# A longer ring of score tiles, one staging place less, and loads of single tiles, in an argmax, gather and scatter kernel

The kernel runs on **one core of one Trainium2 chip**. The metric is the device time of one execution in microseconds (us); lower is better.

## The reference

```python
B, S, H = (8, 2048, 2560)          # fp32; scores (B,S,S), values (B,S,H)
best_j = np.argmax(scores, axis=2)
gathered = values[b_idx, best_j, :].copy()
out = np.zeros_like(values)
np.add.at(out, (b_idx, best_j, slice(None)), gathered)
```

So every output row is its own row of `values`, times the number of score rows whose argmax hit it. Rows hit once are copied, rows never hit are zeroed, rows hit twice or more are gathered, scaled and scattered. No value crosses to another row.

## The kernel before

VectorE finds the argmax of each score row tile (128 rows of 2048), 16 tiles in a batch, 8 batches. TensorE counts the hits. From the counts come lists of rows, and GpSimd issues indirect DMAs from these lists: **copies** from DRAM to DRAM (16 in a batch, of some 47 real rows each), **zeros** from a row of zeros in SBUF (7 in a batch, 12 in the last), and five **gathers** into staging places, five ScalarE scalings and five **scatters**. Loads of scores go through the hardware queue (q1), all the indirect transfers through GpSimd's software queue (q0).

Score tiles go through a ring: a fixed row of places that the loads fill in turn, each as soon as VectorE has scanned the tile that lay there. Score tiles and staging places share one SBUF region, `room`. At the start the first two turns of the score ring also use most of the staging area.

```python
    R = 4; NV = 6; NX = NV * H // S; NB = 14       # NX = 7
    ZCAP, MCAP = 7, 5
    ...
    room = ctx.enter_context(nc.sbuf_tensor([P, NV * H + NB * S], FP32))
    turn = NX + NB                                 # 21 tiles
    def place(x):
        return NV * H + (x % turn - NX if x < 2 * turn else (x - 2 * turn) % NB) * S

    loads, x = {}, 0
    while x < B * NT:
        n = 1
        most_n = 1 if x < 2 or 2 * turn - 6 <= x < 2 * turn else 2 if x < 4 or 2 * turn <= x < 4 * NT else R
        while n < most_n and (x + n) % NT and place(x + n) == place(x) + n * S:
            n += 1
        loads[x] = n                               # n tiles in one DMA
        x += n
    ...
        # per batch, as soon as the counts are there:
        first = (NT, 6, 4)[min(b, 2)]              # copies that need only the counts
        for t in range(first):
            copy_once(t)
        ...                                        # the lists are made
        rest = list(range(first, NT))
        def gathers():
            for k in range(MCAP):
                v = stage()                        # next of NV staging places
                gather(v, mi[:, k:k + 1])
                nc.scalar.activation(out=v, in_=v, ..., scale=mc[:, k:k + 1])
                staged.append(v)
                if rest:
                    copy_once(rest.pop(0))
        def zeros(columns):
            for k in columns:
                scatter(zrow[:], zi[:, k:k + 1], free_running)
                if rest:
                    copy_once(rest.pop(0))
        nz = ZLAST if b == B - 1 else ZCAP
        if b == 0:
            zeros(range(nz))
            while tiles[0] < turn + NX:
                yield
            gathers()
        else:
            gathers()
            zeros(range(ZHEAD))
        for k in range(MCAP):
            scatter(staged[k], mi[:, k:k + 1], ...)
        if b > 0:
            zeros(range(ZHEAD, nz))
```

Of the kernel before, what the change touches and what calls it, by code (L numbers as in the profile page):

```python
# [10 lines left out]
FP16 = mybir.dt.float16  # L11
# [3 lines left out]
P = 128  # L15
# [21 lines left out]
def kernel(  # L37
# [7 lines left out]
    B, S, S2 = scores.shape  # L45
    _, _, H = values.shape
    assert S == S2
    NT = S // P
    BIG = float(1 << 24)
    R = 4  # L50
    G = 4
    NV = 6
    NX = NV * H // S
    NB = 14
    NM = NT // 2
    NE = 16
    LE = P // NE
# [11 lines left out]
    fin = ctx.enter_context(tc.tile_pool(name="fin", bufs=2))  # L69
    ohp = ctx.enter_context(tc.tile_pool(name="ohp", bufs=1))  # L70
# [47 lines left out]
    zrow = ctx.enter_context(nc.sbuf_tensor([P, H], FP32))  # L118
    nc.scalar.copy(zrow[:], zero1[:].to_broadcast([P, H]))


    room = ctx.enter_context(nc.sbuf_tensor([P, NV * H + NB * S], FP32))
    nc.scalar.copy(room[:, 0:NV * H - NX * S], zero1[:].to_broadcast([P, NV * H - NX * S]))
    turn = NX + NB

    def place(x):

        return NV * H + (x % turn - NX if x < 2 * turn else (x - 2 * turn) % NB) * S


    loads, x = {}, 0
    while x < B * NT:
        n = 1
        most_n = 1 if x < 2 or 2 * turn - 6 <= x < 2 * turn else 2 if x < 4 or 2 * turn <= x < 4 * NT else R
        while n < most_n and (x + n) % NT and place(x + n) == place(x) + n * S:
            n += 1
        loads[x] = n
        x += n
# [30 lines left out]
    def scatter(v, idx, note=writes_out):  # L169
        note(nc.gpsimd.indirect_dma_start(  # L170
            out=out_flat[:, :], out_offset=bass.IndirectOffsetOnAxis(ap=idx, axis=0),
            in_=v, in_offset=None, bounds_check=B * S - 1, oob_is_err=False))

    vslot = [0]
    tiles = [0]

    def stage():
        v = room[:, vslot[0] * H:(vslot[0] + 1) * H]
        vslot[0] = (vslot[0] + 1) % NV
        return v  # L180

    def count_steps(b, cnt_ps):

        am = None
        for t in range(NT):
            x = b * NT + t
            if x in loads:
                n = loads[x]
                nc.sync.dma_start(out=room[:, place(x):place(x) + n * S],
                                  in_=scores[b, t * P:(t + n) * P, :].rearrange("(p r) s -> p (r s)", r=n))  # L190
            g = t % G
            if g == 0:
                am = small.tile([P, G, 8], U32, name="am")
            rows = room[:, place(x):place(x) + S]
            mx = small.tile([P, 8], FP32)
            nc.vector.max(out=mx[:], in_=rows)  # L196
# [81 lines left out]
    def value_steps(b, cnt_ps):  # L278
# [12 lines left out]
        def copy_once(t):  # L291
            free_running(scatter_rows_in_dram(
                nc, out_flat[:, :], values[b, t * P:(t + 1) * P, :], one_i[:, t:t + 1], last_row))
# [28 lines left out]
        if b == B - 1:  # L322
# [9 lines left out]
            out=oh[:], in0=lo[:].unsqueeze(2).to_broadcast([P, NT, P]),  # L332
            in1=fill_f[:].unsqueeze(1).to_broadcast([P, NT, P]), op=ALU.is_equal)

        ez = fin.tile([P, NT, NT], FP16)
        nc.vector.tensor_tensor(  # L336
            out=ez[:], in0=hi[:, 0, :].unsqueeze(2).to_broadcast([P, NT, NT]),
            in1=lane_f[:, 0:NT].unsqueeze(1).to_broadcast([P, NT, NT]), op=ALU.is_equal)
        em = fin.tile([P, NT, NM], FP16)
        nc.vector.tensor_tensor(  # L340
            out=em[:], in0=hi[:, 1, :].unsqueeze(2).to_broadcast([P, NT, NM]),
            in1=lane_f[:, 0:NM].unsqueeze(1).to_broadcast([P, NT, NM]), op=ALU.is_equal)
        put = fin.tile([P, NT, 2 * NM + NT], FP16)
        nc.vector.tensor_tensor(out=put[:, :, 0:NM], in0=em[:], in1=row1_f[:].unsqueeze(2).to_broadcast([P, NT, NM]), op=ALU.mult)  # L344
        nc.vector.tensor_tensor(out=put[:, :, NM:2 * NM], in0=em[:], in1=cnt[:].unsqueeze(2).to_broadcast([P, NT, NM]), op=ALU.mult)
        nc.vector.tensor_tensor(out=put[:, :, 2 * NM:], in0=ez[:], in1=row1_f[:].unsqueeze(2).to_broadcast([P, NT, NT]), op=ALU.mult)  # L346
# [19 lines left out]
        def gathers():  # L366
            for k in range(MCAP):
                v = stage()
                gather(v, mi[:, k:k + 1])
                nc.scalar.activation(out=v, in_=v, func=mybir.ActivationFunctionType.Copy, bias=0.0,  # L370
                                     scale=mc[:, k:k + 1])
# [10 lines that stand above are left out]

        nz = ZLAST if b == B - 1 else ZCAP
        if b == 0:
            zeros(range(nz))

            while tiles[0] < turn + NX:
                yield
            gathers()
        else:  # L390
            gathers()
            zeros(range(ZHEAD))
        for k in range(MCAP):

            scatter(staged[k], mi[:, k:k + 1], writes_out if b * MCAP + k < B * MCAP - NV else free_running)
        if b > 0:
            zeros(range(ZHEAD, nz))
        assert not rest
# [3 lines left out]
    with tc.manual_schedule(engines={ET.PE, ET.DVE, ET.Activation, ET.SP}):  # L402
        pending = iter(())
        for b in range(B):
            cnt_ps = psum_c.tile([P, NT], FP32)
            for _ in count_steps(b, cnt_ps):
                next(pending, None)
            for _ in pending:
                pass
            pending = value_steps(b, cnt_ps)  # L410
            for _ in range((1, 4, 0)[min(b, 2)]):
                next(pending)
        for _ in pending:
            pass
        full = fin.tile([1, 2], FP32)
        nc.vector.tensor_reduce(out=full[:, 0:1], in_=tots[0:1, 0, 0:B - 1], op=ALU.max, axis=mybir.AxisListType.X)
        nc.vector.tensor_reduce(out=full[:, 1:2], in_=tots[0:1, 1, :], op=ALU.max, axis=mybir.AxisListType.X)
        over = fin.tile([1, 3], FP32)
        nc.vector.tensor_single_scalar(out=over[:, 0:1], in_=full[:, 0:1], scalar=float(ZCAP * P), op=ALU.is_gt)
        nc.vector.tensor_single_scalar(out=over[:, 1:2], in_=full[:, 1:2], scalar=float(MCAP * P), op=ALU.is_gt)  # L420
        nc.vector.tensor_single_scalar(out=over[:, 2:3], in_=most[0:1, :], scalar=float(ZLAST * LE), op=ALU.is_gt)
        over_i = fin.tile([1, 1], INT32)
        nc.vector.tensor_reduce(out=over_i[:], in_=over[:], op=ALU.max, axis=mybir.AxisListType.X)
# [69 lines left out]
```

## Time and profile before

| | before |
|---|---|
| median of three runs | 828.0 us (827.82 to 829.2) |
| profiled run | 827.44 us, span 825.6 us |
| bytes moved | 347.04 MB, 420 GB/s over the span |
| VectorE | 679.0 us busy, idle after some 697 us |

### The profile page before, as it was taken

The page shows a single profiled execution, that of the slowest core. Times are in us where ns is not written, and L with a number is a line of the kernel's source. Part 1 is how long each engine was busy: PE and PEld are TensorE (multiplying, and loading weights), DVE is VectorE, ACT ScalarE, POOL GpSimd, SP SyncE. Part 2 cuts the span into 40 slices and gives each one's busy share as a digit, 9 for nine tenths or more (in the row PEclk, how much of TensorE's full clock was granted, in tenths as well). Part 3 has the DMA queues.
Part 4 walks back from the last instruction along what each step waited for, and adds up shares of the span by engine and source line. Part 5 has one row for each costly group of instructions (what it writes and reads, how often), then busy time and mean ns, then how long its engine had stood idle before and what let it go on. Part 6 is the DMA issues. An engine that isn't in the chain of part 4 may idle for free.

```text
span 825.6 us, 2045 instructions
## 1 busy us (share of the span) xinstructions
PE 14.7 (2%) x273; PEld 14.1 (2%) x273; DVE 679.0 (82%) x794; ACT 101.2 (12%) x43; POOL 274.7 (33%) x277
## 2 busy tenths in 40 slices
PE   0000000000000000000000000000000000000000
PEld 0000000000000000000000000000000000000000
DVE  7999999999999999999999999999999996000000
ACT  2000000500220002210002300013100320230230
POOL 0000651266121260152501343501505266346351
DMA  9999999999999999999999999999999999999997
GB/s 384 432 431 429 413 409 423 392 410 413 426 429 427 423 431 431 427 424 432 420 428 429 439 419 431 419 436 430 430 415 421 425 426 423 425 427 422 424 426 313
DMA packets 45664, 347.04 MB, mean 420 GB/s; under 512 B 18742, under 2 KB 18742, under 8 KB 18742
## 3 DMA queue, kind: packets, MB, share of 16 engines
q0 software_dynamic: 38736, 212.67, 62.1%
q1 hardware_dynamic: 6912, 134.22, 38.1%
q14 instruction: 14, 0.11, 0.0%
q8 instruction: 2, 0.03, 0.0%
HBM read 354.42 MB, written 300.15 MB: 793 GB/s over the span
## 4 chain that ended last, share of the span: by engine, by line
DVE 71%; DMA 13%; issue 8%; POOL 5%; another core or an unknown queue 1%; POOLq 0%; PE 0%; DVEq 0%
DVE am L197 32%; DVE mx L196 30%; DMA room<-in_values_dram,many_i 8%; DMA out_dram<-room,many_i 4%; POOL out_dram L33 2%; DVE oh_lo L204 2%; POOL out_dram L170 2%; DVE oh L331 2%; POOL room L165 1%; DMA room<-in_scores_dram 1%; DVE lo L200 1%; DVE oh_hi L208 0%; DVE hi L202 0%; DVE put L346 0%
## 5 line engine op out<-in xcount | busy, mean ns | idle before, releaser
L196 DVE MAX8 mx<-room 128x8 f32<-128x2048 f32 x128 | 291.7, 2279 | 4.6 <-DMA room<-in_scores_dram 4.6
L197 DVE FIND_INDEX8 am<-mx,room 128x8 uint32<-128x2048 f32 x128 | 292.4, 2285 | 0.0
L370 ACT ACTIVATE room<-room,many_c 128x2560 f32<-128x2560 f32 x40 | 96.7, 2426 | 693.0 <-DMA room<-in_values_dram,many_i 693.0
L33 POOL DMA_INDIRECT out_dram<-in_values_dram,ones_i x128 | 131.2, 1025 | 145.7 <-DVE m L302 107.7
L170 POOL DMA_INDIRECT out_dram<-room,many_i x40 | 39.7, 994 | 248.2 <-ACT room L370 248.2
L165 POOL DMA_INDIRECT room<-in_values_dram,many_i x40 | 41.8, 1046 | 122.2 <-DMA out_dram<-room,many_i 73.9
L170 POOL DMA_INDIRECT out_dram<-zrow,zero_i x61 | 60.8, 996 | 18.8 <-issue 18.8
L204 DVE TENSOR_TENSOR oh_lo<-lo,lane_f 128x512 bf16<-128x512 uint32 x32 | 22.1, 692 | 0.3
L331 DVE TENSOR_TENSOR oh<-lo,fill_f 128x2048 f16<-128x2048 uint32 x8 | 18.3, 2291 | 0.3
L212 PE MATMUL cnt_ps<-oh_hi,oh_lo 128*128 128x16 bf16 x128 | 8.1, 174 | 572.9 <-DVE oh_hi L208 528.7
L212 PEld LDWEIGHTS <-oh_lo 128*128 128x128 bf16 x128 | 8.4, 105 | 572.7 <-DVE oh_lo L204 547.3
L197 DVE MATCH_VALUE_LOAD am<-mx,room 128x8 f32 x128 | 11.8, 92 | 4.3
L208 DVE TENSOR_TENSOR oh_hi<-hi,lane_f 128x64 bf16<-128x64 uint32 x32 | 7.0, 218 | 0.0
L200 DVE TENSOR_SCALAR lo<-am 128x4 uint32<-128x4 uint32 x32 | 5.7, 178 | 1.1
L349 PE MATMUL l_ps<-put,oh 128*128 128x32 f16 x128 | 4.7, 188 | 73.4 <-DVE put L346 73.4
L349 PEld LDWEIGHTS <-oh 128*128 128x128 f16 x128 | 4.7, 104 | 74.5 <-DVE oh L331 64.1
L202 DVE TENSOR_SCALAR hi<-am 128x4 uint32<-128x4 uint32 x32 | 5.5, 172 | 0.0
L336 DVE TENSOR_TENSOR ez<-hi,lane_f 128x256 f16<-128x256 uint32 x8 | 3.3, 417 | 0.0
L346 DVE TENSOR_TENSOR put<-ez,row_f 128x256 f16<-128x256 f16 x8 | 3.3, 417 | 0.0
L321 DVE TENSOR_SCALAR rank<-base,off_ps 128x16 f32<-128x16 f32 x16 | 3.2, 244 | 0.0
L358 DVE TENSOR_SCALAR e<-l_ps 128x32 f32<-128x32 f32 x8 | 1.5, 184 | 2.0 <-PE l_ps L349 2.0
L344 DVE TENSOR_TENSOR put<-em,row_f 128x128 f16<-128x128 f16 x8 | 2.4, 298 | 0.3
(88 smaller groups left out, 53.5 us busy)
## 6 DMA issues: line engine op xcount, KB each, us to landing
room<-in_scores_dram SPq DMA_DIRECT2D x20, 4096.0 KB, 23.6
room<-in_scores_dram SPq DMA_DIRECT2D x18, 2048.0 KB, 11.7
room<-in_scores_dram SPq DMA_DIRECT2D x9, 1024.0 KB, 8.4
room<-in_scores_dram SPq DMA_DIRECT2D x1, 3072.0 KB
out_dram<-in_values_dram,ones_i POOLq DMA_INDIRECT x128
out_dram<-zrow,zero_i POOLq DMA_INDIRECT x61
room<-in_values_dram,many_i POOLq DMA_INDIRECT x40, 33.3
out_dram<-room,many_i POOLq DMA_INDIRECT x40, 51.4
```

The costliest lines, as they stand in the source:

```text
L33: return eng.add_instruction(ins)
L165: note(nc.gpsimd.indirect_dma_start(out=v, out_offset=None, in_=values_flat[:, :], in_offset=bass.IndirectOffsetOnAxis(ap=idx, axis=0), bo ...
L170: note(nc.gpsimd.indirect_dma_start(out=out_flat[:, :], out_offset=bass.IndirectOffsetOnAxis(ap=idx, axis=0), in_=v, in_offset=None, bound ...
L196: nc.vector.max(out=mx[:], in_=rows)
L197: nc.vector.max_index(out=am[:, g, :], in_max=mx[:], in_values=rows)
L200: nc.vector.tensor_single_scalar(out=lo[:], in_=am[:, :, 0], scalar=P - 1, op=ALU.bitwise_and)
L204: nc.vector.tensor_tensor(out=oh_lo[:], in0=lo[:].unsqueeze(2).to_broadcast([P, G, P]), in1=lane_f[:].unsqueeze(1).to_broadcast([P, G, P]) ...
L208: nc.vector.tensor_tensor(out=oh_hi[:], in0=hi[:].unsqueeze(2).to_broadcast([P, G, NT]), in1=lane_f[:, 0:NT].unsqueeze(1).to_broadcast([P, ...
L212: nc.tensor.matmul(out=cnt_ps[:], lhsT=oh_lo[:, k, :], rhs=oh_hi[:, k, :], start=(t == G - 1 and k == 0), stop=(t == NT - 1 and k == G - 1))
L331: nc.vector.tensor_tensor(out=oh[:], in0=lo[:].unsqueeze(2).to_broadcast([P, NT, P]), in1=fill_f[:].unsqueeze(1).to_broadcast([P, NT, P]), ...
L349: nc.tensor.matmul(out=l_ps[:], lhsT=oh[:, t, :], rhs=put[:, t, :], start=(t == 0), stop=(t == NT - 1))
L370: nc.scalar.activation(out=v, in_=v, func=mybir.ActivationFunctionType.Copy, bias=0.0, scale=mc[:, k:k + 1])
```

## The change

It is meant to close the hole at 150 to 170 us by giving the ring more tiles and freeing one staging place early. The ring has 22 tiles at first and 16 afterwards (before 21 and 14). There are five staging places, not six, and the first overlaps no score tile of the second turn, so its gather can go early. Tiles 22 to 47 (most of batches 1 and 2) are loaded one at a time (singles), later ones in pairs (to tile 79) and fours, each one DMA. In batch 0 two zero columns go after the first two scatters.

```diff
-    NV = 6
+    NV = 5
     NX = NV * H // S
-    NB = 14
+    NY = 4
+    NB = 16
...
-        return NV * H + (x % turn - NX if x < 2 * turn else (x - 2 * turn) % NB) * S
+        y = x - NX if x < turn else x - turn - NY if x < turn + NY else (x - turn - NY) % NB
+        return NV * H + y * S
...
-        most_n = 1 if x < 2 or 2 * turn - 6 <= x < 2 * turn else 2 if x < 4 or 2 * turn <= x < 4 * NT else R
+        most_n = 1 if x < 2 or turn <= x < 3 * NT else 2 if x < 4 or turn <= x < 5 * NT else R
...
-        ez = fin.tile([P, NT, NT], FP16)
+        ez = ohp.tile([P, NT, NT], FP16)          # em and put likewise: a pool of one buffer
...
         if b == 0:
-            zeros(range(nz))
-            while tiles[0] < turn + NX:
+            zeros(range(nz - 2))
+            while tiles[0] < turn + NY:
                 yield
             gathers()
...
             scatter(staged[k], ...)
+            if b == 0:
+                zeros(range(nz - 2 + k, min(nz - 1 + k, nz)))
```

More of the change, by code (lines that the diff above doesn't have):

```diff
@@ L338, in value_steps @@
             in1=lane_f[:, 0:NT].unsqueeze(1).to_broadcast([P, NT, NT]), op=ALU.is_equal)
-        em = fin.tile([P, NT, NM], FP16)
+        em = ohp.tile([P, NT, NM], FP16)
         nc.vector.tensor_tensor(
@@ L342, in value_steps @@
             in1=lane_f[:, 0:NM].unsqueeze(1).to_broadcast([P, NT, NM]), op=ALU.is_equal)
-        put = fin.tile([P, NT, 2 * NM + NT], FP16)
+        put = ohp.tile([P, NT, 2 * NM + NT], FP16)
         nc.vector.tensor_tensor(out=put[:, :, 0:NM], in0=em[:], in1=row1_f[:].unsqueeze(2).to_broadcast([P, NT, NM]), op=ALU.mult)
```

## The prediction

> **What bounds the kernel now.** I read the page's 40 slices and queues first, then windows of 10 us, then the timelines around the weak windows.
>
> ```profile
> span 825.6 us, 2045 instructions
> DVE  7999999999999999999999999999999996000000
> DMA  9999999999999999999999999999999999999997
> q0 software_dynamic: 38736, 212.67, 62.1%
> q1 hardware_dynamic: 6912, 134.22, 38.1%
> ```
>
> VectorE looks full, but it ends near 697 us (timeline) and 130 us of transfers follow. The DMA row is full throughout, and the two queues' packet times add up to the span (62.1% + 38.1%): q1 loads scores, q0 does the indirect copies, zero rows, gathers and scatters. So the chain of waits, which gives DVE 71%, misleads. What counts is bytes, packet cost and holes in the DMA row. The page's 347.04 MB at 425 GB/s, the rate of the undisturbed windows, take 817 us. Some 9 us of the span are start, drain and holes; the windows say where.
>
> ```profile
> core 0: us, PE busy (x) PEld busy (x) DVE busy (x) ACT busy (x) POOL busy (x), PEclk, DMA share, GB/s
> 90.00:100.00 10.00, 0.59 (x16) 0.58 (x16) 9.79 (x17) 0.00 (x0) 8.17 (x7) 1.00 0.99 408
> 100.00:110.00 10.00, 0.00 (x0) 0.00 (x0) 9.90 (x11) 0.00 (x0) 7.57 (x9) 1.00 1.02 388
> ...
> 150.00:160.00 10.00, 0.25 (x4) 0.26 (x4) 9.93 (x9) 7.28 (x3) 2.11 (x3) 1.00 0.93 390
> 160.00:170.00 10.00, 0.25 (x4) 0.26 (x4) 9.53 (x10) 4.75 (x2) 2.77 (x3) 1.00 0.99 373
> ...
> 180.00:190.00 10.00, 0.00 (x0) 0.00 (x0) 9.90 (x9) 0.00 (x0) 7.56 (x9) 1.00 1.03 393
> ...
> 700.00:710.00 10.00, 0.00 (x0) 0.00 (x0) 0.00 (x0) 0.00 (x0) 6.90 (x8) 1.00 1.02 426
> ```
>
> The last two columns matter. Seven windows between 90 and 200 us lie 10 to 52 GB/s under 425: these five by 17, 37, 35, 52 and 32, and 120 to 130 and 190 to 200 by 10 and 16. The sum of 199 over 425, times 10 us, is **4.7 us**: all that a better order could win there. Later windows average 425. The timelines tell the cause at 150 us:
>
> ```profile
> 135.59 0.99 POOL L165 DMA_INDIRECT room<-in_values_dram,many_i  x1 [9.26 <-DVE am L197]
> 140.18 0.99 POOL L165 DMA_INDIRECT room<-in_values_dram,many_i  x1 [3.60 <-DVE am L197]
> 144.77 0.99 POOL L165 DMA_INDIRECT room<-in_values_dram,many_i  x1 [3.60 <-DVE am L197]
> 153.84 1.00 POOL L170 DMA_INDIRECT out_dram<-room,many_i  x1 [8.08 <-ACT room L370]
> ```
>
> The first gathers stand behind VectorE, because score tiles still lie in the staging places. The first scatter follows only at 153.84. Meanwhile q1 has nothing: in the trace's packet records no score byte moves for some 33 us before about 160 us. The pair of tiles 42 and 43 goes to the places of tiles 28 and 29 (ring of 14), and VectorE finishes 29 at 159.3. So q0 runs dry with q1 empty.
>
> **What the Trainium skill says.** "DMA: Bandwidth & Descriptors", section Where 436 GB/s comes from, gives a port ceiling of 435 GB/s. The trace agrees: windows of loads alone reach 419 to 442, so no order raises the rate much. Its section Issuing engines are not separate DMA queues says that all issuers share 16 engines and interleave; the two shares that sum to 100% agree. Its Rules for kernel authors ask for at least 1 MiB per DMA; a single row tile is just that (1024 KB). In the packet records 8192 B take 309 ns, 16384 B 611, 24576 B 916 and 32768 B 1213: a single costs 2% more per byte than a batch of four[...].
>
> **The change part by part.** The rebuilt order has the same instructions on PE, DVE and ACT; SP gets 17 more loads and POOL two rows more in another order. Bytes do not change.
>
> 1. Loads. Counted from the load plan: before 9 singles, 18 pairs, 1 triple, 20 fours; after 28, 24, 0, 13. Each has 128 packets over 16 engines, so 8 times the packet time: before 8 x (9 x 309 + 18 x 611 + 916 + 20 x 1213) ns = 311.6 us, after 8 x (28 x 309 + 24 x 611 + 13 x 1213) = 312.7 us. On the bound: **+1.1 us**.
>
> 2. The hole at 150 to 170 us (87 GB/s x 10 us / 425 = 2.0 us). The new places make gathers 1 to 4 wait for tiles 22, 23, 24, 25, and gather 0 for none. The timeline has VectorE through with them at 125.0, 129.7, 135.2 and 139.8; gather 0 can issue at 115, after five zero scatters instead of seven. Before they issued at 121, 125, 136, 140 and 145. A zero column of some 113 rows (an estimate: 753 rows unhit, 5 x 128 taken off) now follows the first scatter and feeds q0 there. Load 42 needs tile 26, done at 144.4, not 29 at 159.3, and then one tile is loaded per tile eaten. Ledger from 144.4 to 171 us, when batch 1 brings new copies: room for 26.6 us x 0.427 = 11.4 MB. Supply: about 3 MB left in q0, scatters 5.5 MB (541 rows, an estimate), the late zero column 1.2, six single loads 6.3: 16 MB. So no dry stretch, and about 4.6 MB of backlog enters batch 1. I take all of it: **-2.0 us**.
>
> 3. The dip at 180 to 200 us (1.1 us): q0 alone, with packets of 0.6 to 1.4 us instead of 0.385. Single loads keep q1 going beside it. I cannot say that this cures slow packets, so half: **-0.5 us**.
>
> 4. The dip at 90 to 130 us (64 x 10 / 425 = 1.5 us): here load x needs tile x - 20 instead of x - 21, so q1 is one tile poorer when copies (some 0.48 MB each, one per 1.28 us, 376 GB/s) start to feed q0. Singles free q1 sooner. No gain, **0 to +0.3 us**.
>
> 5. Five staging places: every gather waits for the scatter of the batch before in the same place. POOL waits there already:
>
> ```profile
> POOL room L165 <- DMA out_dram<-room,many_i: 73.9, 16, 21.5
> ```
>
> There will be more such waits, up to 35. But behind a landing scatter stand the later scatters, three zeros and seven copies, some 20 us of transfers, so the DMA does not notice. At the end POOL's last scatter (795.20) may come 4 to 6 us later, while 11 us of transfers are queued. **0 us**, with a small risk.
>
> 6. Moving three small tiles to a pool of one buffer: each is written once a batch, and PE reads it within 5 us. **0 us**.
>
> Sum: +1.1 - 2.0 - 0.5 + 0.1 = -1.3 us, so **826.7 us** from 828.0.
>
> **Rivals.** (a) The hole moves: VectorE frees a tile only every 4.6 to 5 us, so the ring may empty q1 elsewhere. For it: part 4's tile less, and the staging area closed at 26 tiles instead of 28. Against it: the ledger's surplus. Time: 828 to 830. (b) Staging binds: the circle of gather (33 us), scaling (2.4), scatter (51.4 median) comes to 87 us, as long as a batch (about 85 us of VectorE). If it held POOL until q0 ran dry, each batch would lose some us: 832 to 845. Against it: both latencies are queueing, and shrink as the queue empties. (c) All dips vanish, slow packets too: 828.0 - 4.7 + 1.1 = 824.4. (d) VectorE becomes the bound if singles land late: it waited only once for a load (4.6 us, at the start), and ends 130 us early. Unlikely.
>
> **Range and chances.** The floor is (c) less 0.9 for the scatter that three runs showed (827.82 to 829.2), 823.5; the top is (a), 829.5. A change of 2% needs 16.6 us: the holes hold 4.7 in all, so faster by 2% is nearly excluded, and slower needs (b) in several batches. Faster 0.01, same 0.97, slower 0.02.
>
> **What would show it.** Right: 150 to 170 us at 420 GB/s or more, first scatter by 147 us instead of 153.84, no stretch over 25 us without score bytes before 160 us, q1 carrying more packets at an unchanged 134.22 MB, VectorE still without waits after the first. POOL's wait for scatters grows while the DMA stays above 0.98. Wrong: more than two windows after 210 us under 410 GB/s (before has two), a tail below 420 before the last 10 us, or slow packets in new places.

## More of the kernel before

The prediction shows the lines that say what bounds it. Two more parts of the page of the kernel before: the GB/s row (40 slices of 20.6 us) and the loads (count, KB of each, us from issue to landing).

```profile
GB/s 384 432 431 429 413 409 423 392 410 413 426 429 427 423 431 431 427 424 432 420 428 429 439 419 431 419 436 430 430 415 421 425 426 423 425 427 422 424 426 313
DMA packets 45664, 347.04 MB, mean 420 GB/s; under 512 B 18742, under 2 KB 18742, under 8 KB 18742
...
room<-in_scores_dram SPq DMA_DIRECT2D x20, 4096.0 KB, 23.6
room<-in_scores_dram SPq DMA_DIRECT2D x18, 2048.0 KB, 11.7
room<-in_scores_dram SPq DMA_DIRECT2D x9, 1024.0 KB, 8.4
room<-in_scores_dram SPq DMA_DIRECT2D x1, 3072.0 KB
```

Besides the first slice, which holds the start, only slices between the fifth and the tenth (83 to 206 us; all but the seventh) lie visibly low, and the last holds the end. There is little to win, and all of it early.

## The result

| | median | lowest to highest | runs |
|---|---|---|---|
| before | 827.91 us | 827.47 to 829.2 | 6 |
| changed | 828.85 us | 828.41 to 829.2 | 6 |

The ratio is 1.0009 (95% interval 0.9996 to 1.0021): the same. The two profiled runs stand at opposite ends of their kernels' runs: 827.44 us for before, near its fastest, and 829.2 us for the changed one, its slowest. The traces therefore differ by 1.8 us of span, the medians only by 0.9.

The page of the changed kernel, parts as before:

```profile
span 827.4 us, 2091 instructions
GB/s 380 437 423 421 404 404 430 424 424 403 425 428 427 428 424 427 427 427 438 418 429 430 425 428 434 417 429 429 435 422 422 423 427 418 425 424 415 423 426 277
DMA packets 48112, 347.04 MB, mean 419 GB/s; under 512 B 19014, under 2 KB 19014, under 8 KB 19014
q1 hardware_dynamic: 9360, 134.22, 38.1%
room<-in_scores_dram SPq DMA_DIRECT2D x13, 4096.0 KB, 48.8
room<-in_scores_dram SPq DMA_DIRECT2D x24, 2048.0 KB, 12.3
room<-in_scores_dram SPq DMA_DIRECT2D x28, 1024.0 KB, 10.6
```

The bytes are the same; q1 has 9360 packets for 6912, as the plan of loads says. In the GB/s row the eighth slice rose from 392 to 424, the fifth fell from 413 to 404, and the last from 313 to 277. The windows of the changed kernel tell it finer (columns as in the prediction; the last two are the DMA share, which is the mean busy share of the 16 DMA engines, and GB/s). The profile counts a packet's time and bytes whole in the window in which it starts. Sixteen packets of 32768 B, one on each engine, are 0.5 MB, or 52 GB/s in a window of 10 us, so windows with loads in fours swing by some tens of GB/s, and shares go over 1. The holes and dips below were checked in the packet records, with the bytes of each packet spread over its time.

```profile
90.00:100.00 10.00, 0.59 (x16) 0.58 (x16) 9.79 (x17) 0.00 (x0) 8.18 (x7) 1.00 1.02 399
100.00:110.00 10.00, 0.00 (x0) 0.00 (x0) 9.90 (x11) 0.00 (x0) 7.57 (x9) 1.00 1.01 383
...
150.00:160.00 10.00, 0.25 (x4) 0.26 (x4) 9.93 (x9) 4.53 (x2) 3.81 (x4) 1.00 1.01 425
160.00:170.00 10.00, 0.23 (x4) 0.26 (x4) 9.58 (x10) 4.86 (x2) 1.49 (x3) 1.00 1.02 427
180.00:190.00 10.00, 0.00 (x0) 0.00 (x0) 9.90 (x9) 0.00 (x0) 7.57 (x9) 1.00 1.02 403
190.00:200.00 10.00, 0.26 (x4) 0.26 (x4) 9.93 (x9) 0.00 (x0) 7.72 (x8) 1.00 1.01 391
750.00:760.00 10.00, 0.00 (x0) 0.00 (x0) 0.00 (x0) 0.00 (x0) 5.85 (x6) 1.00 1.01 406
```

And two windows of the kernel before that the prediction doesn't show:

```profile
190.00:200.00 10.00, 0.25 (x4) 0.26 (x4) 9.90 (x10) 0.00 (x0) 7.57 (x8) 1.00 1.00 409
...
750.00:760.00 10.00, 0.00 (x0) 0.00 (x0) 0.00 (x0) 0.00 (x0) 6.00 (x6) 1.00 1.02 422
```

The hole at 150 to 170 us is gone (390 and 373 became 425 and 427). The dip at 180 to 200 us is not: its low half moved from the first window (393, now 403) to the second (409, now 391). There is a new dip in the tail (422, now 406).

GpSimd's part of the timeline of the changed kernel:

```profile
115.02 1.04 POOL L166 DMA_INDIRECT room<-in_values_dram,many_i  x1 [0.30 <-issue]
125.33 1.00 POOL L166 DMA_INDIRECT room<-in_values_dram,many_i  x1 [9.26 <-DVE am L198]
...
140.23 0.99 POOL L166 DMA_INDIRECT room<-in_values_dram,many_i  x1 [3.60 <-DVE am L198]
152.38 1.00 POOL L171 DMA_INDIRECT out_dram<-room,many_i  x1 [11.16 <-ACT room L371]
...
752.29 1.04 POOL L166 DMA_INDIRECT room<-in_values_dram,many_i  x1 [5.08 <-DMA out_dram<-room,many_i]
```

The gathers went when the prediction said (115, 125, 129.7, 139.8). The first scatter did not: 152.38 us, only 1.46 us earlier than before, because it waits for the scaling, and the scaling for a gather that lands late behind other transfers. At 752.29 a gather waited 5.08 us for the scatter in its staging place; in the kernel before the longest such wait between 746 and 761 us was 1.90. In the list of waits:

```profile
POOL room L166 <- DMA out_dram<-room,many_i: 79.0, 18, 20.0
```

against 73.9 us and 16 waits before: little more, not the "up to 35".

### Where the 1.8 us between the traces come from

From the packet records (one record for each packet, with its queue, size, start and duration) I summed the bytes that had moved by each time, and took the changed kernel's lead over the kernel before, in us at 425 GB/s (my own bookkeeping):

| up to | lead of the changed kernel | step since the row above |
|---|---|---|
| 90 us | -0.5 us | -0.5: loads alone, singles against fours |
| 150 us | -1.1 | -0.6: dip at 90 to 120 us deeper |
| 170 us | +1.0 | **+2.1: the hole filled** |
| 210 us | +0.65 | -0.35: dip at 180 to 200 us |
| 680 us | +0.67 | 0.0: six batches alike |
| 810 us | 0.0 | -0.7: the tail, most of it at 690 to 700 and 750 to 760 us |
| end | -1.7 | **-1.7: the drain** |

The last row needs a word. With 2 MB left both kernels stand within 0.2 us of each other, at 815.7 and 815.9 us. Then the number of packets in flight falls from 16 to none, and it does so sooner and more slowly in the changed kernel. Summed over the last 16 us before the last byte, the share of the 16 DMA engines that stood idle is worth 3.4 us before and 5.1 us after. The last byte lands at 823.8 and 825.5 us. I call this end the drain. So the engines end unevenly, and nothing is left that could fill the engines that are done.

### The profile page after: what moved, and what is told of

The parts are those of the page before. It is cut to its first block, busy times and chain, and to the rows that moved or that the text cites. A ratio compares the mean times of both kernels' runs of the same rounds, so it can differ in the third digit from the quotient of the medians.

```text
span 827.4 us, 2091 instructions
## 1 busy us (share of the span) xinstructions
PE 14.7 (2%) x273; PEld 14.2 (2%) x273; DVE 679.0 (82%) x794; ACT 100.7 (12%) x43; POOL 273.0 (33%) x277
## 3 DMA queue, kind: packets, MB, share of 16 engines
q1 hardware_dynamic: 9360, 134.22, 38.1%
## 4 chain that ended last, share of the span: by engine, by line
DVE 81%; DMA 12%; issue 3%; POOL 2%; PE 0%; POOLq 0%; DVEq 0%
DVE am L198 37%; DVE mx L197 34%; DMA room<-in_values_dram,many_i 7%; DMA out_dram<-room,many_i 4%; DVE oh_lo L205 3%; DVE oh L332 2%; POOL out_dram L171 1%; POOL out_dram L33 1%; DVE lo L201 1%; DMA room<-in_scores_dram 1%; DVE oh_hi L209 1%; POOL room L166 0%; DVE hi L203 0%; DVE rank L322 0%; DVE put L347 0%
```

## The experiments

**Theories.** The letters appear in the expectations below.

- **H**: a stretch of DRAM-to-DRAM copies with no other transfers beside it runs below 425 GB/s although the DMA share is full; the dips at 90 to 130 and 180 to 200 us are such stretches, so the order of copies matters, not the ring.
- **P**: finer loads cost what their packet times say (1.1 us here), on the bound.
- **R**: the hole was filled by the ring and the loads. Its rival **Z**: by the zero column that now comes after the first scatter.
- **Staging**: five places hold GpSimd back.
- **S** (rival of H): the early dip is a short queue; copies arrive too slowly to keep the engines full.

For every run I worked out three numbers against the profiled run of before: the lead at 810 us, the extra idleness in the drain, and the span. Lead and drain together give the span within 0.4 us in nine of the twelve rows (e6 is off by 0.45, e7 by 0.8 and e12 by 1.0, most of which lies after the last byte: from there to the end of the program are 1.9 us in the kernel before and 2.3, 2.6 and 2.7 us in these three; e3, whose lead at a fixed time says less, is left out):

| run | lead at 810 us | drain, more idle | span against 825.6 | median | ratio to before (95%) |
|---|---|---|---|---|---|
| changed | 0.0 | 1.7 | +1.8 | 828.85 | 1.0009 (0.9996 to 1.0021) |
| e1 | -2.2 | 0.7 | +3.0 | 830.37 | 1.0024 (1.001 to 1.0038) |
| e2 | -1.0 | 0.9 | +1.9 | 829.68 | 1.0018 (1.0004 to 1.0032) |
| e4 | +1.2 | 0.3 | -0.8 | 826.62 | 0.998 (0.9966 to 0.9994) |
| e5 | -1.0 | 1.5 | +2.5 | 829.57 | 1.0014 (0.9996 to 1.0032) |
| e6 | -0.25 | -0.5 | +0.2 | 827.91 | 0.9992 (0.9977 to 1.0008) |
| e7 | -3.2 | 0.6 | +4.6 | 831.75 | 1.0035 (1.0019 to 1.005) |
| e8 | +0.5 | 0.85 | +0.4 | 828.23 | 0.9998 (0.9985 to 1.001) |
| e9 | +1.3 | 1.05 | -0.3 | 827.19 | 0.9975 (0.9962 to 0.9989) |
| e10 | -2.1 | 0.1 | +2.6 | 829.83 | 1.0003 (0.9989 to 1.0017) |
| e11 | -0.2 | 1.2 | +1.5 | 827.77 | 0.9983 (0.9969 to 0.9996) |
| e12 | -0.2 | -0.5 | +0.7 | 827.22 | 0.9975 (0.9959 to 0.999) |

The kernel before ran beside each group, on another chip each time: 828.04 (e1 to e4), 828.55 (e5 to e8) and 828.88 us (e9 to e12), median. Single runs of it reached 831.47, so the ratio is the safer column. All these rows are in the class "same", as no ratio is 2% from 1. The drain column comes from one trace per kernel, so I cannot say how much of it repeats.

### e1: the changed kernel with singles only for tiles 36 to 47

```diff
-        most_n = 1 if x < 2 or turn <= x < 3 * NT else 2 if x < 4 or turn <= x < 5 * NT else R
+        most_n = 1 if x < 2 or turn + 14 <= x < 3 * NT else 2 if x < 4 else R
```

> The changed kernel with fewer load packets: tiles 22 to 35 and everything from tile 48 on in fours where the places run on, singles only for tiles 36 to 47. The sum of packet times is then that of the kernel before (311.6 us instead of 312.7), the order of the ring unchanged. Theory P (the finer loads cost what their packets take on a full DMA): about 1.0 us less than the changed kernel, 827.8 against 828.85, with the loss of 0.5 us that the changed kernel shows between 60 and 90 us gone. Rival Q (the singles are what fills the hole at 150 to 170 us, or packet size does not matter): no gain, 828.9 or more, or the hole back.

Measured 830.37 us. By 70 us it leads the changed kernel by 0.35 us, as P says, but then comes a hole. Window of e1:

```profile
80.00:90.00 10.00, 0.45 (x6) 0.40 (x6) 9.34 (x22) 0.00 (x0) 3.38 (x4) 1.00 0.66 256
```

The kernel before has 424 GB/s there. The batch of tiles 32 to 35 needs the place of the last of four tiles, and VectorE is done with that (tile 15) only at 83.2 us. Meanwhile nothing else is there to move, because the first copies have just been issued. It costs 4 us. So singles are worth having at 80 to 90 us: they hold q1 up where q0 has not begun. I had not seen this use of them, and my expectation of 827.8 us missed. The hole at 150 to 170 us stays filled (427 and 425).

### e2: the changed kernel with all 128 tiles loaded singly

```diff
+        most_n = 1
```

> The changed kernel with every load a single row tile: 128 loads, packet times 316.4 us instead of 312.7. Theory P: +3.7 us, about 832.6. If small packets only cost where they stand alone on the DMA (first 86 us) and hide beside the indirect queue: under +1 us, about 829.5.

Measured 829.68 us, 0.8 above the changed kernel in the medians. P's time, 832.6 us, missed, and the rival's 829.5 came out, but not because the cost hides. The cost is seen and is not small: e2 falls back by 1.0 us against the changed kernel in the first 60 us and by 1.8 between 200 and 620 us. But the dips are shallower (416 and 424 GB/s at 180 to 200 us, 419 at 90 to 100), which gives back 1.1 and 0.6. Packet cost of single loads is real where loads run alone or steadily. It is bought back where copies stand in a stretch, by my reading because more load packets run beside them.

### e3: the changed kernel with all copies of a batch issued first

```diff
-        first = (NT, 6, 4)[min(b, 2)]
+        first = NT
```

> The changed kernel with all 16 copies of rows hit once in a row at the start of every batch, as batch 0 has them, instead of 4 or 6 in a row and the rest between gathers and zero scatters. Bytes and packets the same. Theory H (a stretch of DRAM-to-DRAM copies one after the other runs the DMA at 350 to 410 GB/s instead of 425, and so makes the dips at 90 to 120 and 180 to 200 us): such dips in every batch, 0.4 to 1.3 us each, in all 3 to 8 us slower, 832 to 837. Rival S (the dips come from GpSimd writing descriptors while the queue is short): batches 2 to 7 have 6 MB and more queued, so no new dips, 828 to 830.

Measured 845.02 us, ratio 1.0202 (1.0186 to 1.0217): 16 us slower than the changed kernel, more than the 3 to 8 that I expected (the interval lies across 2%, so the class is "unclear", though not the direction). Windows of e3 in the tail batches:

```profile
640.00:650.00 10.00, 0.25 (x4) 0.26 (x4) 9.90 (x11) 0.00 (x0) 7.85 (x8) 1.00 1.04 346
650.00:660.00 10.00, 0.00 (x0) 0.00 (x0) 9.93 (x7) 0.00 (x0) 5.44 (x6) 1.00 1.00 362
...
710.00:720.00 10.00, 0.00 (x0) 0.00 (x0) 0.00 (x0) 0.00 (x0) 7.64 (x8) 1.00 1.04 349
```

The share is full and the rate 15 to 19% low: the engines are not short of work, each packet takes longer. Packets of 10240 B that took over 0.6 us (the usual is 0.385) number 245, against 68 in the changed kernel; their mean is 397.5 ns against 387.4, which over 20762 packets on 16 engines makes 13 of the 15.4 us that e3 lags at 810 us. Within a stretch the first four copies or so still run at some 390 to 424 GB/s; the later ones average 345 (642 to 658 and 708 to 724 us). It is not a matter of issuing: in batch 5 the slow copies had been issued 13 us earlier, in batch 3 52 us, with 4.7 to 10 MB queued. In batches 1 and 2, where loads run beside the copies, hardly anything is lost. H holds for these stretches: S expected 828 to 830.

### e4: the changed kernel with ten copies first in batch 0 and four in batch 1

```diff
-        first = (NT, 6, 4)[min(b, 2)]
+        first = (10, 4, 4)[min(b, 2)]
```

> The changed kernel with shorter stretches of copies in batches 0 and 1: 10 instead of 16 in a row in batch 0 (the other six between zero scatters and the first gather), 4 instead of 6 in batch 1. Theory H: the dips at 90 to 120 and 180 to 200 us shrink, 0.7 to 1.5 us less than the changed kernel, about 827.7. Rival S: unchanged, 828.5 to 829.2.

Measured 826.62 us (826.4 to 826.88), 2.2 below the changed kernel and below the kernel before. Windows of e4:

```profile
100.00:110.00 10.00, 0.00 (x0) 0.00 (x0) 9.90 (x11) 0.00 (x0) 7.13 (x8) 1.00 1.01 379
180.00:190.00 10.00, 0.00 (x0) 0.00 (x0) 9.90 (x9) 0.00 (x0) 6.57 (x8) 1.00 1.03 424
190.00:200.00 10.00, 0.25 (x4) 0.26 (x4) 9.91 (x9) 0.00 (x0) 7.87 (x8) 1.00 1.01 419
```

The dip at 180 to 200 us is cured (403 and 391 became 424 and 419), by order alone; whether by the four copies of batch 1 or by what moved in batch 0 was not separated. The one at 100 to 110 us is not. Its lead at 810 us is 1.2 us; the other 1.4 us that separate its trace from the changed kernel's lie in the drain.

### e5: the changed kernel with all zero columns ahead of the gathers

```diff
-            zeros(range(nz - 2))
+            zeros(range(nz))
...
-            if b == 0:
-                zeros(range(nz - 2 + k, min(nz - 1 + k, nz)))
```

> The changed kernel with all seven zero columns of batch 0 ahead of the gathers, as the kernel before has them; ring, staging and loads as changed. Theory R (the single loads that the ring of 16 lets through from tile 42 on fill the hole at 150 to 170 us): the hole stays filled, 420 GB/s or more in both windows, 829. Rival Z (the zero column kept back feeds the queue there): a dip of 10 to 40 GB/s in these windows, +0.5 to +1.5 us.

Measured 829.57 us. Windows of e5:

```profile
150.00:160.00 10.00, 0.26 (x4) 0.27 (x4) 9.93 (x9) 2.43 (x1) 1.00 (x1) 1.00 1.01 426
160.00:170.00 10.00, 0.23 (x4) 0.26 (x4) 9.58 (x10) 4.86 (x2) 0.99 (x1) 1.00 1.01 423
180.00:190.00 10.00, 0.00 (x0) 0.00 (x0) 9.90 (x9) 0.00 (x0) 7.63 (x8) 1.00 0.99 368
```

The hole stays filled: R, not Z. (The column in question has 121 rows, 1.2 MB.) But the next dip is deeper (368 instead of 403), so the late zeros were worth something there: 0.7 us by 210 us.

### e6: the kernel before with tiles 42 to 47 loaded singly

```diff
-        most_n = 1 if x < 2 or 2 * turn - 6 <= x < 2 * turn else 2 if x < 4 or 2 * turn <= x < 4 * NT else R
+        most_n = 1 if x < 2 or 2 * turn - 6 <= x < 3 * NT else 2 if x < 4 or 2 * turn <= x < 4 * NT else R
```

> The kernel before with tiles 42 to 47 loaded singly instead of in pairs; ring of 14 and six staging places kept. Load 42 then waits for tile 28 (154.7 us) instead of 29 (159.3). Theory R: about half of the hole is filled, as the load starts 4.6 us sooner: 826.9 to 827.5, 0.5 to 1.1 us under the kernel before. If the ring's size is not what matters: the hole is gone or unchanged.

Measured 827.91 us, within the scatter of before. At 170 us its trace leads by 0.65 us, as R says; at 810 us it is 0.25 behind. Windows of e6:

```profile
150.00:160.00 10.00, 0.26 (x4) 0.26 (x4) 9.93 (x8) 7.29 (x3) 2.13 (x3) 1.00 0.94 367
160.00:170.00 10.00, 0.26 (x4) 0.26 (x4) 9.51 (x11) 4.86 (x2) 2.76 (x3) 1.00 1.01 424
```

The second half of the hole is filled, the first is not. Singles help only once the place's former tile is done; the rest needs a load that waits for an earlier tile. The longer ring gives one, and so, in another way, does e7.

### e7: the kernel before with five staging places and nothing else

```diff
-    NV = 6
+    NV = 5
```

> The kernel before with five staging places instead of six and nothing else (the first ring shrinks from 21 to 20 tiles with it). Step 5 of the prediction (the longer waits for scatters cost nothing, as the queue behind them is deep): 827.5 to 828.5 apart from what the first 21 tiles lose, at most 1 us. Rival b (staging binds): a DMA share under 0.95 or a rate under 400 GB/s in windows of batches 2 to 7, and 830 or more.

Measured 831.75 us. Window of e7:

```profile
80.00:90.00 10.00, 0.45 (x6) 0.39 (x6) 9.34 (x22) 0.00 (x0) 3.37 (x4) 1.00 0.67 259
```

This is the hole of e1 again (the first ring has 20 tiles here, and loads come in fours): 4.3 us, where I expected at most 1. The hole at 150 to 170 us vanishes (426 and 424), since the loads there now need earlier tiles. No full window of batches 2 to 7 falls below 400 GB/s or a share of 0.95, so Staging does not bind in the steady part; rival b's time (830 or more) was reached by the smaller first ring. The hole also fills here with a later ring of only 14, so it is not the ring's size as such that counts, but for which tile the loads at 150 us wait.

### e8: the changed kernel with the lists of batch 0 made early and only four copies first

```diff
+        first = 4
...
-            for _ in range((1, 4, 0)[min(b, 2)]):
+            for _ in range((3, 4, 0)[min(b, 2)]):
```

> The changed kernel with VectorE making batch 0's lists before it scans tile 16 (zero list ready near 92 us instead of 100.9), and only four copies in a row at the start of batches 0 and 1, the rest one by one between zero scatters and gathers. Theory H (stretches of more than about four copies run at 320 to 400 GB/s): the dips at 90 to 120 and 180 to 200 us are gone, 2 to 3 us less than the changed kernel, 825.5 to 826.7. Rival S (writing descriptors while the queue is short is what costs): the dip at 90 to 110 stays, 827 or more.

Measured 828.23 us. The early dip only moved: 371 GB/s at 90 to 100 us, 412 and 398 after it (399, 383, 410 in the changed kernel). GpSimd took 2.38 us over the third of its four copies (at 88.43 us), and q0 ran short: from 90 to 100 us idle engines cost 0.5 us and long packets 0.8 us, against 0.2 and 0.5 in the changed kernel. So S is at work too, for the smaller part. It is not peculiar to e8: in the changed kernel and in e4 one copy, at 92.33 and 92.41 us, took 3.09 us, while most others come 1.28 us apart. The packets stayed long although from 93.59 to 105.16 us copies and zero columns were issued in turn. Neither theory as it stands explains the early dip. The later one shrank (422 and 407 at 180 to 200 us), as H says; the time that H expected, 825.5 to 826.7, missed.

### e9: e4 with singles only for tiles 30 to 47

```diff
+        most_n = 1 if x < 2 or turn + 8 <= x < 3 * NT else 2 if x < 4 else R
+        first = (10, 4, 4)[min(b, 2)]
```

> The kernel e4_copies_mixed with single loads only for tiles 0, 1 and 30 to 47 and fours elsewhere where places run on (packet times 311.9 us instead of 312.7). Theory P: 0.8 us under e4_copies_mixed, about 825.8, with no hole at 80 to 90 us, as the singles start before the queue of loads runs out there. If the start of singles at tile 30 is too late: a hole at 80 to 90 us and 828 or more.

Measured 827.19 us, ratio 0.9975. There is no hole at 80 to 90 us (421 GB/s), and it is 0.5 us ahead of e4 by 80 us, as P says. But e4 has made that up by 210 us, and e9 is no faster in the end; my 825.8 missed.

### e10: the kernel before with the order of copies of e4

```diff
-        first = (NT, 6, 4)[min(b, 2)]
+        first = (10, 4, 4)[min(b, 2)]
```

> The kernel before with only the copies mixed: 10 instead of 16 in a row in batch 0, 4 instead of 6 in batch 1. Theory H: the dips at 90 to 120 and 180 to 200 us shrink here as in e4_copies_mixed, 1 to 2 us under the kernel before, 826 to 827; the hole at 150 to 170 us stays. Rival: order matters only with the changed ring, no gain.

Measured 829.83 us, ratio 1.0003: no gain, where H expected 1 to 2 us. Two windows of e10:

```profile
280.00:290.00 10.00, 0.25 (x4) 0.26 (x4) 9.86 (x15) 0.00 (x0) 6.03 (x6) 1.00 1.02 405
290.00:300.00 10.00, 0.00 (x0) 0.00 (x0) 9.93 (x7) 0.00 (x0) 7.58 (x8) 1.00 1.04 406
```

The kernel before has 416 and 447 in these. With four copies first in batch 1, its last two copies end up next to the first four of batch 2, with only a zero column of some nine rows between. By my reading the stretch was moved by 100 us, not taken apart. In e4 the same six copies have loads beside them and run at 433 and 417. The lead falls by 1.2 us from 280 to 300 us. So mixing the copies paid only with the changed kernel's loads, and the hole at 150 to 170 us (391, 374) stays too.

### e11 and e12: copies also after the scatters, with the loads of e4 and of e9

```diff
+        first = (10, 4, 2)[min(b, 2)]
...
             scatter(staged[k], mi[:, k:k + 1], ...)
+            if rest:
+                copy_once(rest.pop(0))
```

> The kernel e4_copies_mixed with the copies spread further: from batch 2 on only two ahead of the gathers, and one after each scatter while any are left. Theory H: the small dips of the tail (690 to 700, 750 to 760 us) go, 0.3 to 0.8 us under e4_copies_mixed, about 826. If the longer hold of copies behind the waits for scaling runs the queue short: 827 or more, with dips before 800 us.

> Both together: copies spread as in e11_mixed_even and loads as in e9_mixed_fours. If the two gains add: about 825.3, under both kernels of the study and under e4_copies_mixed (826.6).

Measured 827.77 and 827.22 us. In e11 the dips in the tail are still there (413 at 680 to 690 us, 410 at 750 to 760), and both are behind e4 and e9 at 810 us by 1.4 to 1.5 us. My expectations of 826 us for e11 and 825.3 for e12 missed. e12 has the evenest drain of the three. e4, e9 and e12 are 0.20 to 0.25% under the kernel before; their order among each other is within the noise.

## Why the prediction was right and where it was wrong

The class (same) and the range held, the size was 2.2 us too low, and the sign was wrong: -1.3 predicted, +0.9 in the medians, +1.8 between the two traces. The class was safe, as the holes held 4.7 us and 2% are 16.6; that the range held is in part luck (see rival (a) below). Step by step:

1. **Loads, +1.1.** Right in kind, and near in size (its own sum is 1.04, not 1.1): 0.5 us in the first 90 us, where loads run alone, and part of the 0.6 that follows. e1 and e2 show the packet cost, e1 also that singles avoid a hole of 4 us at 80 to 90 us, which the step did not name.
2. **The hole, -2.0.** Right in size, 2.1 us, but the cause was only half right, so the size is in part luck. The prediction takes the whole hole for a lack of work, with q0 dry and q1 empty. The packet records show that for 150 to 160 us: idle engines cost 0.9 us. From 160 to 170 us the prediction's own line has a share of 0.99 at 373 GB/s: engines were hardly idle (0.1 us), and 1.1 us went to long packets (loads of 16384 B that start at 158 to 172 us took 713 ns on average, not 611). The change removed both parts; why packets are long there stays open. The gathers were issued on time, and q1's pause shrank from 37 us (125 to 162; the prediction's 33 was misread) to 17 us (131 to 148). The first scatter by 147 us was wrong (152.38), because a gather landed later than the ledger had it. The filling did not need it, nor the late zeros (e5): the loads carried it.
3. **The dip at 180 to 200 us, -0.5.** Wrong: +0.35. The step counted on single loads to keep q1 going beside q0. They did not: no load packet started from 178.7 to 191.0 us (180.1 to 190.9 before). Taking the copies apart cured the dip (e4).
4. **The dip at 90 to 130 us, 0 to +0.3.** The direction was right, the size too small: 0.6 by 150 us (0.9 at 120 us) together with the rest of step 1, which the sum cannot tell apart.
5. **Five staging places, 0.** This step failed in the tail only. The argument, that transfers lie queued behind each wait, held in the six batches between (lead 0.65 at 210, 0.67 at 680 us). In the tail 0.7 us are lost, among others in the window where GpSimd waited 5.08 us. By my bookkeeping of issued less served bytes q0 still held more than 3 MB then, so it was not the queue running dry; in that window (750 to 760 us) idle engines cost 0.1 us more than in the kernel before, and long packets 0.3. That the wait changed what stood next to what, and that this costs the 0.7 us, is argued, not shown.
6. **Small tiles moved, 0.** Nothing contradicts it: VectorE's only wait for a load is still the first (4.5 us).
7. **What the sum left out: the end.** 1.7 us of the traces' difference lie after 810 us, nearly all of them in the last 2 MB, in the uneven end of the 16 DMA engines. I had the window from 810 us on in view for both queues and asked only when the last scatter is issued. The drain cost between 2.9 us (e6) and 5.1 us (the changed kernel) in the profiles from before to e12 other than e3, as much as the holes that I argued about. Whether the changed kernel always drains badly stays open: there is one trace of it, of its slowest run. If the lead of 0.0 at 810 us repeats, the medians leave some 0.9 us for the drain.

The total is then 0.5 + 0.6 - 2.1 + 0.35 + 0.7 + 1.7 = 1.75 us, against 1.8 measured between the traces.

Rival (c), all dips vanish, was ruled out by the windows. Rival (b) did not occur. Rival (a) named the right range, 828 to 830, by another cause: the hole did not move within q1, its gain was spent elsewhere. The top of the range, 829.5, came from (a). Of the prediction's own signs of being wrong, two came true: a tail below 420 GB/s (415 at 690 to 700 us, 406 at 750 to 760) and slow packets in a new place (750 to 760 us). The prediction also miscounted: before has three windows under 410 GB/s between 210 and 810 us (407, 407, 401), not two. And its 419 to 442 GB/s for windows of loads alone are swings of the kind described under the result; the window at 10 to 20 us even shows 462. Loads alone average 430 GB/s from 20 to 90 us in the kernel before and 427 in the changed one, which is under the 435 that it cites.

**How far H goes.** The Trainium skill, "HBM Reference", section Specifications (TRN2), gives about 716 GB/s for one HBM domain and says that a core streaming alone reaches about 425, bounded by its DMA engines. The trace agrees with the second: 425 to 429 for gathers alone and 428 to 429 for zeros alone. A copied byte is read from HBM and written to HBM, so the 345 GB/s of the later copies in e3 are 690 GB/s there, close to the first figure (an estimate from that page). That is a coincidence of numbers, not a proof. Four things do not fit. The first four copies of a stretch run at nearly full rate. What runs beside the last copies of a stretch and behind them is slow too (328 GB/s over both queues at 192 to 195 us in the changed kernel). Packets are long at 160 to 170 us in the kernel before, although GpSimd issued no copy between 107.37 and 171.08 us. And in the tail of the kernel before, some five copies in a row ran at 422 to 424. What the chip is short of in a stretch stays open. That order alone makes and removes such losses is shown by e3 (new ones) and by e4 (the dip at 180 to 200 us); the dip at 90 to 120 us yielded to no order that was tried.

## What to carry to other kernels

When the DMA is full from end to end, a hole closed in one place is worth its bytes only if nothing further down spends them: follow the cumulative bytes to the last byte, and look at how many engines are still busy in the last 10 us. A window with a full share and a low rate is no lack of work but slow packets; change what runs side by side, and try not to put many transfers from DRAM to DRAM in a row (here e3 lost 15 us so). A finer load costs its packets (2% per byte here) and pays where its queue would otherwise stand empty.

## What the Trainium skill lacked or had wrong

- "DMA: Bandwidth & Descriptors", section Where 436 GB/s comes from: its note says that for transfers between HBM and SBUF the HBM side, about 358 GB/s, binds. That is a core's share with both cores of a pair running; with one core running, loads alone averaged 430 GB/s (20 to 90 us) and the whole kernel 420. "HBM Reference" has it right.
- The same page, section Rules for kernel authors, asks for at least 1 MiB per DMA. It lacks what a DMA of that size costs when others are in flight: 309 ns for 8192 B, 611 for 16384 B, 1213 for 32768 B, so 2% per byte between singles and fours; all 128 tiles loaded singly (e2) cost 0.8 us of 829 on balance.
- No page that I read says that the rate falls within a run of direct DRAM-to-DRAM copies: 345 GB/s after the first four or so in e3, which lags by 15.4 us at 810 us.
- No page that I read says what it costs that the 16 engines finish apart at the end of a kernel: idle engines were worth 2.9 to 5.1 us in the last 16 us (before to e12, without e3).
